# Gates of a hybrid decoder block computed by block products in a stage of their own, with three projections and the gated linear unit put in other places

## The chip, the cores and the metric

One core of a Trainium2 chip runs the whole program in a single launch. The metric is the device time of one execution in microseconds (us). The engines are named as the profile names them: PE (matrix multiply, with PEld for its weight loads), DVE (vector), ACT (scalar), POOL (GpSimd) and SP, which issues most of the transfers. Each engine works through its own queue in order.

## The reference, cut to what matters

One decoder block of width 1024 over 1024 tokens, in float32. After an RMS norm `u`, one projection gives the state space input, q, k, v, forget logits and two sets of gate logits:

```python
proj = u @ w_in[l]
u_ssm, q, k, v, f_logit, gate_logits = jnp.split(proj, [...], axis=-1)
y_ssm = jax.nn.gelu(s5_ssm(u_ssm, ...))                  # diagonal state space, 32 groups
glu_a, glu_b = jnp.split(y_ssm @ w_glu[l], 2, axis=-1)
out_a = glu_a * jax.nn.sigmoid(glu_b)
att = forgetting_attention(q, k, v, f_logit + b_forget)  # 8 heads of 64, causal
gate_a, gate_b = jnp.split(jax.nn.sigmoid(gate_logits), 2, axis=-1)
h = h + (gate_a * out_a + gate_b * (att @ w_fox_o)) @ w_mix_out
```

Then come a cross attention into 256 memory tokens, a gated feed-forward layer and a last norm, which the change leaves as they are.

## The kernel before, in words

Every matrix is held as a rounded high part and a low part (`split`, L172: ACT writes the high part, DVE subtracts it from the source for the low part), and a product is three matmuls, high by high, high by low and low by high (`mm3`, L161). A block of weights is 128x1024: it is loaded into `raw` (2 buffers) and split into `whi` and `wlo` (4 buffers each). The order of instructions on each engine is worked out when the program is built, by a list scheduler with a cost model; the order in the code is the priority. So an instruction may run ahead of its place in the code when its inputs and its buffer are free, and each engine's queue is then fixed.

The stages around the change:

1. `stage_in` (L327) norms the input, turns it into `uT` (transposed, high and low, 16 tiles of 128x1024), and stores the state space input `u_d`.
2. `stage_ssm` (L441) works the state space off in four quarters. For a quarter `weights` (L1161, POOL and DVE) builds tables, `turn_weights` (L1221) and `states` (L1245) run small matmuls on PE, a chain of DVE operations with two scans, and `out` (L1288) the last matmuls, a GELU on ACT and a split on DVE; `store` (L1305) sends the result to `y_d` in 16 transfers. Beside it PE computes the gates: 32 halves (16 blocks of 128 gates, 2 halves of 512 tokens, L447), each of 24 matmuls of 128x512, a sigmoid on ACT (L453) and a store to `gate_d` from ACT's queue (L454). `todo` (L460) says before which half each step of the state space stands.
3. `values_of_v` (L1328) projects v, 16 times 24 matmuls of 256 or 264 columns.
4. `run` (L1569): q and k of a head come from one weight block (`project`, L1425, 48 matmuls a head), those of heads 0 and 1 ahead of the loop, those of heads 2 to 7 between the 12 units (128 keys by up to 512 queries) of earlier heads. A unit does scores (L1508, L1509), the causal mask on DVE, the exponential on ACT (L1515), the split of the result (L1517 to L1521), and the products with v. `row_max` (L1466) finds the maxima of the next head on DVE. Beside head 7 run the first halves of the gated linear unit (`Glu.values`, L1004) for 4 of its 8 blocks.
5. `stage_tail` (L471) begins with the rest of the gated linear unit (`Glu.rest`, L1007: a product, a sigmoid on ACT, a product of both on DVE, L995, and one with the gate on POOL, L1002) and with `fox_part` (L493), the output projection of the attention, its gate and the sum. Then come mixing, cross attention and feed-forward.

The feed-forward layer already multiplies by seven block products (L719 to L804): two neighbouring 128-wide column blocks and two halves of the tokens make a 2x2 block product of which seven products of 12 matmuls each are taken in place of eight, with sums of weight blocks (`w_sums`, L740, on DVE) and of input blocks (`norm_blocks`, L686).

Memory is given out in pools that open and close like brackets. A pool that opens later lies where closed ones lay, and its tile waits for the last use of the tiles that lay there.

## Time and profile before

| | us |
|---|---|
| median of 3 runs (1609.87 to 1611.17) | 1610.64 |
| the profiled execution's own time | 1611.79 |
| its span in the profile | 1610.1 |
| busy: PE, DVE, ACT, POOL | 1543.0, 1019.0, 647.7, 254.6 |
| mean granted clock of PE | 0.982 |

The profile is of one execution. A table by windows gives for each stretch of time how long each engine was busy, the clock that PE was granted and how busy the transfer engines were. A group of instructions has a line, an engine, an operation, tiles (written from read), a shape, a count, and then busy time and mean duration. Matmuls are pipelined: a row may say 0.39 us for one while the next starts 0.23 us later, so time on PE is counted from start to start.

### The profile page before, as it was taken

How to read it: one execution, taken by the hardware profiler on the slowest of the kernel's cores; microseconds unless marked ns; L12 is line 12 of the kernel's file. 1: busy time of each engine (PE TensorE's matmuls, PEld its weight loads, DVE VectorE, ACT ScalarE, POOL GpSimd, SP SyncE). 2: the span in 40 equal slices, each digit the busy share in tenths (PEclk: the TensorE clock that was granted, in tenths of full speed). 3: DMA queues.
4: the chain of work that ended last, by engine and by line, in shares of the span. 5: the costliest groups of instructions: out<-in, count | busy, mean ns of one | idle time of the engine just before them, and what ended most of it. 6: DMA issues, size and time to landing. Idle time of an engine off the chain costs nothing.

```text
span 1610.1 us, 20541 instructions
## 1 busy us (share of the span) xinstructions
PE 1543.0 (96%) x7313; PEld 1267.3 (79%) x7313; DVE 1019.0 (63%) x1850; ACT 647.7 (40%) x1169; POOL 254.6 (16%) x339
## 2 busy tenths in 40 slices
PE   7799799998999999999999989999999999999997
PEld 6588688898677668888888776888888888888886
DVE  6655665424778776764355697776777667565555
ACT  6322333323566653222235574333333333344342
POOL 2025545100111112310001200000010000000001
PEclk8899999999899999999999999999999999999999
DMA  7746656633322453544203155444455544896642
GB/s 262 125 77 120 92 118 104 152 69 42 41 54 61 120 156 89 168 131 144 92 3 103 57 193 181 159 151 152 156 161 165 167 155 141 274 392 228 194 157 105
DMA packets 226102, 221.77 MB, mean 138 GB/s; under 512 B 50872, under 2 KB 159512, under 8 KB 226000
## 3 DMA queue, kind: packets, MB, share of 16 engines
q1 hardware_dynamic: 221392, 212.08, 47.1%
q10 hardware_dynamic: 4608, 8.39, 1.4%
q8 instruction: 57, 0.93, 0.2%
q14 instruction: 45, 0.37, 0.1%
HBM read 154.06 MB, written 64.32 MB: 136 GB/s over the span
## 4 chain that ended last, share of the span: by engine, by line
PE 79%; DVE 8%; DMA 6%; ACT 3%; POOL 2%; issue 2%; SPq 0%; DVEq 0%; POOLq 0%; ACTq 0%
PE mm L768 14%; PE pv L768 7%; PE mm L163 7%; PE mm L164 7%; PE mm L165 7%; PE mm L907 5%; PE sc L907 4%; PE sc L768 3%; DMA raw<-in_w_in_dram 3%; PE sc L163 3%; PE sc L165 3%; PE sc L164 3%; PE pv L907 3%; PE misc L907 2%; DVE wlo L174 1%
## 5 line engine op out<-in xcount | busy, mean ns | idle before, releaser
L174 DVE TENSOR_TENSOR wlo<-raw,whi 128x1024 fp32r<-128x1024 f32 (+2 forms) x126 | 133.2, 1059 | 179.6 <-ACT whi L173 166.9
L173 ACT CAST whi<-raw 128x1024 fp32r<-128x1024 f32 (+2 forms) x129 | 116.1, 903 | 303.5 <-DMA raw<-in_w_in_dram 67.9
L163 PE MATMUL mm<-uh,whi 128*128 128x512 f32 x344 | 139.9, 407 | 0.3 <-DVE mc L1486 0.3
L164 PE MATMUL mm<-ul,whi 128*128 128x512 f32 x344 | 137.9, 401 | 0.0
L165 PE MATMUL mm<-uh,wlo 128*128 128x512 f32 x344 | 137.6, 400 | 0.0
L174 DVE TENSOR_TENSOR ol<-or,oh 128x1024 fp32r<-128x1024 f32 x73 | 89.3, 1223 | 70.2 <-ACT oh L173 69.1
L173 ACT CAST oh<-or 128x1024 fp32r<-128x1024 f32 x73 | 76.8, 1053 | 103.7 <-PE mm L907 33.3
L800 POOL TENSOR_TENSOR g<-a,c 128x512 f32<-128x512 f32 x22 | 35.3, 1606 | 391.7 <-ACT a L799 357.4
L165 PEld LDWEIGHTS mm<-uh,wlo 128*128 128x128 f32 x344 | 66.6, 194 | 14.0 <-DVE wlo L174 0.7
L163 PEld LDWEIGHTS mm<-uh,whi 128*128 128x128 f32 x344 | 66.4, 193 | 12.8 <-DVE mc L1486 0.6
L164 PEld LDWEIGHTS mm<-ul,whi 128*128 128x128 f32 x344 | 66.5, 193 | 11.7
L1518 POOL TENSOR_TENSOR pl<-pf,ph 128x512 fp32r<-128x512 f32 (+1 forms) x32 | 36.9, 1153 | 236.6 <-DVE ph L1517 222.6
L192 POOL TENSOR_TENSOR r<-ms,mhalf 128x1 f32<-128x1 f32 x26 | 17.5, 672 | 359.0 <-DVE ms L188 350.7
L1515 ACT ACTIVATE pf<-sc 128x512 f32<-128x512 f32 (+1 forms) x96 | 46.4, 490 | 50.2 <-DVE sc L1511 35.1
L768 PE MATMUL pv<-S3h,we 128*128 128x512 f32 x176 | 58.9, 394 | 2.7 <-ACT S3h L173 2.7
L907 PE MATMUL mm<-oh 128*128 128x512 f32 x106 | 41.2, 389 | 0.0
L907 PE MATMUL mm<-ol,oh 128*128 128x512 f32 x106 | 41.2, 389 | 0.0
L907 PE MATMUL mm<-oh,ol 128*128 128x512 f32 x106 | 41.2, 389 | 0.0
L1521 DVE TENSOR_TENSOR pl<-pf,ph 128x512 fp32r<-128x512 f32 (+2 forms) x64 | 36.4, 571 | 7.6 <-ACT ph L1520 6.8
L768 PEld LDWEIGHTS pv<-S3h,we 128*128 128x128 f32 x176 | 33.3, 189 | 10.0 <-ACT S3h L173 3.1
L163 PE MATMUL sc<-uh,whi 128*128 128x512 f32 x104 | 40.8, 393 | 0.0
L1002 POOL TENSOR_TENSOR sg<-sg,ga 128x512 f32<-128x512 f32 x16 | 29.2, 1847 | 72.9 <-DVE sg L995 72.5
(574 smaller groups left out, 4556.5 us busy)
## 6 DMA issues: line engine op xcount, KB each, us to landing
or<-c_d SPq DMA_DIRECT2D x77, 256.0 KB
raw<-in_w_ffn_in_dram SPq DMA_DIRECT2D x22, 512.0 KB
rawb<-in_w_ffn_in_dram SPq DMA_DIRECT2D x22, 512.0 KB
wo<-in_w_ffn_out_dram SPq DMA_DIRECT2D x22, 512.0 KB
c_d<-g SPq DMA_DIRECT2D x44, 256.0 KB
t_d<-wo SPq DMA_DIRECT2D x44, 256.0 KB
or<-t_d SPq DMA_DIRECT2D x44, 256.0 KB
raw<-in_w_in_dram SPq DMA_DIRECT2D x20, 512.0 KB
```

Of the source, the lines that this page charges most:

```text
L163: T.matmul(ps, lh, rh, start=first, stop=False)
L164: T.matmul(ps, lh, rl, start=False, stop=False)
L165: T.matmul(ps, ll, rh, start=False, stop=last)
L173: self.A.copy(hi, src)
L174: (self.G if pool_lo else self.V).tensor_sub(lo, src, f32(hi))
L768: T.matmul(ps, l_[:, k, :], r_, start=first and k == 0 and i == 0, stop=k == 3 and i == 2, skip_group_check=True)
L800: G.tensor_mul(g[:, 512:], a1, c1)
L907: T.matmul(ps, l_[:, gi], r_[:, 512:], start=n < 3 and p == 0 and k == 0 or n == 7 and p == 0 and k == 0, stop=p == NP - 1 and k == 2, ski ...
L1002: self.B.G.tensor_mul(self.out[j][:, cs], self.out[j][:, cs], ga)
L1515: A.activation(pf[:, off:], ps[:, off:], AF.Exp)
L1518: G.tensor_sub(pl[:, off:], pf[:, off:], f32(ph[:, off:]))
L1521: V.tensor_sub(pl[:, off:], pf[:, off:], f32(ph[:, off:]))
```

## The change

The change does four things.

- **Beside the state space** run v (8 units of two token tiles) and then q and k (8 blocks by 2 halves of tokens). Their high and low parts go to memory (`vh_d`, `vl_d`, `q_d`, `k_d`) from SP's queue, and the attention loads them from there, per head and in two halves. The forget logits are summed at the end of this stage.
- **Gates** come after the state space in `stage_gates`, by seven block products per pair of blocks. The class `Seven` holds the weight side, taken over from the feed-forward layer, which now uses it too. `combine` makes the sums of the input blocks from `uT` in two parts.
- **The gated linear unit** of blocks 0 to 6 is cut into 112 steps of three matmuls: 16 ahead of the attention's loop and one in each of its 96 units. Block 7 comes after the attention. The results go to memory (`sg_d`) and are loaded in the tail.
- The loading of `y_d` moves into and behind the gates, and a few tiles share memory.

```diff
-    gates = [lambda j=j, h=h: gate(j, h) for j in range(16) for h in range(2)]
+    def value(b, t):
+        n = 264 if b else 256
+        ps = B.bank()
+        for k in range(8):
+            wh, wl = wv[b][k // 4]
+            B.mm3(ps[:, :n], *uT.tok(k, t), wh[:, k % 4, :], wl[:, k % 4, :], k == 0, k == 7)
+        hi, lo = parts()
...
+        A.copy(hv[:, :, 0:64], src)
+        V.tensor_sub(lo[:, :256].rearrange("p (h d) -> p h d", h=4), src, f32(hv[:, :, 0:64]))
+        S.dma_start(vh_d[t // 2, :, t % 2, 4 * b:4 * b + 4, :], f32(hv))
+        S.dma_start(vl_d[t // 2, :, t % 2, 256 * b:256 * b + 256], f32(lo[:, :256]))
+    def qk(i, hf):
+        ps = B.bank()
+        B.gemm_t(ps, *wq[i], uT, hf, 8)
+        hi, lo = parts()
...
+        for two in range(2):
+            d_ = (q_d, k_d)[i % 2][i // 2 * 2 + two]
+            h = slice(DH * two, DH * two + DH)
+            S.dma_start(d_[0:DH, cs], f32(first[h, :]))
+            S.dma_start(d_[DH:P, cs], f32(second[h, :]))
+    units = [lambda b=b, t=t: v_unit(b, t) for b in (1, 0) for t in range(0, NT, 2)]
+    units += [lambda i=i, hf=hf: qk_unit(i, hf) for i in range(8) for hf in range(2)]
     for q in range(4):
-        todo[4 + 7 * q] = [lambda q=q: s5.turn_weights(q)]
-        todo[5 + 7 * q] = [lambda q=q: s5.states(q, u_d)] + ([lambda q=q: s5.weights(q + 1)] if q < 3 else [])
-        todo[9 + 7 * q] = [lambda q=q: s5.out(q), lambda q=q: s5.store(q, y_d)]
+        t0 = (4, 10, 15, 21)[q]
+        todo.setdefault(t0, []).append(lambda q=q: s5.turn_weights(q))
+        todo.setdefault(t0 + 1, []).extend([lambda q=q: s5.states(q, u_d)] + ([lambda q=q: s5.weights(q + 1)] if q < 3 else []))
+        todo.setdefault(t0 + 5, []).extend([lambda q=q: s5.out(q), lambda q=q: s5.store(q, y_d)])
...
+    forget.log_forget()
+    forget.cumulate()
+def stage_gates(B, cp, gp, uT, w_in, gate_d, load_y):
+    def slot(dt=F32, name="w"):
+        return gp.tile([P, D], dt, tag="w", bufs=6, name=name)
...
+    def combine(k):
+        for n in ("A11", "A21", "A22"):
+            hi, lo = flat(n)
+            whole[n] = slot(name="f")
+            V.tensor_add(whole[n], f32(hi), f32(lo))
...
+        V.tensor_sub(s1, s1, s3)
+        V.tensor_sub(s3, t, s3)
+        V.tensor_add(t, t, s1)
+        put("S2", t, neg=True)
+        put("S3", s3)
+        put("S1", s1)
+        V.tensor_sub(s4, t, f32(hi))
+        V.tensor_sub(s4, s4, f32(lo))
+        put("S4", s4)
...
+    sv.fetch(0)
+    sv.first(0)
+    sv.fetch(1)
+    start(0)
+    combine(0)
+    sv.first(1)
+    start(1)
+    combine(1)
+    sv.sums(0)
+    sv.last(0)
+    middle(0)
+    end(0)
...
+    for j in range(2, 8):
+        start(j)
+        end(j - 1)
+        sv.last(j)
+        middle(j)
...
+    def steps(self, j, tile_, half):
+        def step(h, b, k):
...
+            B.mm3(ps, wh[:, 4 * b + k, :], wl[:, 4 * b + k, :], *self.yT.rhs(k, h), k == 0, k == 3)
+            if k < 3:
+                return
...
+            if b == 0:
+                B.V.tensor_copy(dst, pv)
+                return
+            sb = half("sb")
+            B.A.activation(sb, ps, AF.Sigmoid)
+            B.V.tensor_mul(dst, dst, sb.rearrange("p (t c) -> p t c", t=4))
...
+        steps = [f for j in range(7) for f in glu.steps(j, big, lambda name: big(name)[:, :512])]
+        weave(steps[:12], self.row_max(0))
+        self.max_row(0)
+        for f in steps[12:16]:
+            f()
+        steps = steps[16:]
...
             if h + 2 < NH:
-                n = 8 if h + 3 == NH else 16
-                for i, f in enumerate(pro[h + 2].parts[:n]):
-                    side[i if n == 8 else PSLOT[i]].append(f)
...
+                side[7].append(lambda: self.load(h + 2, (0,)))
+                side[11].append(lambda: self.load(h + 2, (1,)))
             for i, u in enumerate(units):
                 self.scores(h, *u)
                 for f in side[i]:
                     f()
+                steps.pop(0)()
```

In `put` each sum is split as everywhere, ACT the high part and DVE the low part. `start(j)` runs products 1 and 2 of a pair (inputs A11 and A12, which are `uT` itself), `middle(j)` products 6, 7 and 5 (inputs S2, S3, S1), `end(j)` products 3 and 4 (S4, A22).

499 lines of the change are left out of this document (268 added, 231 removed).

## The prediction

> **What bounds the kernel now.** First the page's engine table:
>
> ```profile
> span 1610.1 us, 20541 instructions
> ...
> PE 1543.0 (96%) x7313; PEld 1267.3 (79%) x7313; DVE 1019.0 (63%) x1850; ACT 647.7 (40%) x1169; POOL 254.6 (16%) x339
> ```
>
> PE is busy for 96% of the span, so a change pays by taking matmuls away or by closing PE's 67 us of idle time. The table by windows shows where these lie in the part that is changed. Its columns are window, length, busy time and count of PE, PEld, DVE, ACT and POOL, granted clock, share of the transfer engines, GB/s.
>
> ```profile
> 113.40:336.50 223.10, 213.96 (x1079) 182.57 (x1078) 112.22 (x150) 75.98 (x120) 100.53 (x201) 0.98 0.64 118
> 336.50:382.00 45.50, 45.09 (x374) 44.52 (x373) 18.27 (x61) 8.73 (x19) 1.64 (x5) 1.00 0.11 20
> 382.00:423.00 41.00, 35.28 (x136) 27.22 (x135) 20.92 (x46) 15.04 (x22) 0.00 (x0) 0.88 0.49 66
> 423.00:474.00 51.00, 49.73 (x245) 37.50 (x244) 38.26 (x98) 34.02 (x67) 9.19 (x8) 1.00 0.25 47
> 474.00:524.00 50.00, 49.45 (x240) 37.08 (x238) 39.76 (x102) 32.18 (x63) 9.24 (x8) 1.00 0.21 55
> 524.00:574.00 50.00, 46.19 (x225) 34.14 (x224) 38.86 (x101) 29.92 (x59) 9.23 (x8) 1.00 0.52 138
> 574.00:624.00 50.00, 47.74 (x228) 35.92 (x228) 36.55 (x71) 24.77 (x51) 9.24 (x8) 1.00 0.36 96
> 624.00:733.00 109.00, 109.00 (x483) 90.23 (x482) 79.18 (x83) 32.51 (x46) 29.20 (x16) 1.00 0.49 152
> ```
>
> These are gates beside the state space, v, the start of attention, its loop (four windows), and the tail to the end of the attention's output projection: 619.6 us. All else stays. The loss in each is idle time plus what the clock took: 9.1 + 0.02 x 214 = 13.4 us in the first, 5.7 + 0.12 x 35 = 9.9 in the third, 7.9 in the loop, nothing in the tail.
>
> The price of a matmul is the step from one start to the next, read from the chain that ended last:
>
> ```profile
> 1019.25 5.44 PE mm L768 x24
> ```
>
> Twenty-four matmuls of 512 columns take 5.44 us, 0.2267 us each. Matmuls of v, with half the columns, take 45.5 / 374 = 0.122 us.
>
> **The change part by part.**
>
> *Matmuls.* The gates fall from 16 x 2 x 24 = 768 matmuls to 8 x 7 x 12 = 672: 96 x 0.2267 = 21.8 us less on PE. v (384), q and k (384) and the gated linear unit (384) keep their counts and only move.
>
> *Beside the state space.* The first window holds 1079 matmuls: 768 for gates (174.1 us), 288 of the state space and 23 early ones of v (2.8 us); with 4.3 us for the clock, the state space takes 213.96 - 174.1 - 2.8 - 4.3 = 32.8 us of PE. After the change PE has, until the last quarter's `states` matmuls end, v (384 x 0.122 = 46.8), 14 of 16 halves of q and k (76.2) and the state space without its last `out` (29.3): 152.3 us. The stalls now:
>
> ```profile
> PE pv L1299 <- DVE St L1285: 5.5, 2, 5.3
> ...
> PE pv L1256 <- ACT F L1229: 3.6, 1, 3.6
> ```
>
> The first is the first quarter's DVE chain: the same number of units stands ahead of its `out`, a little longer ones, so it shrinks. The second comes with a crowded transfer queue:
>
> ```profile
> q10 hardware_dynamic: 4533, 8.27, 9.8%
> ```
> ```profile
> L1309 SPq DMA_DIRECT2D y_d<-yh x32: 302/432/4677, 190.7 to 330.2; - x32
> ```
>
> Queue q10 carried the gates' 32 stores from ACT. In their place SP gets 32 stores of v and 64 of q and k, 12.6 MB, at about 0.43 us an issue 41 us of its time, in a shorter stage. They stand in SP's queue among weight loads, the state space's transfers and `y_d`; a late one holds a `ph` or `pl` buffer (2 each), then ACT, then a PSUM bank. I take 10 us of stalls, between 3 (the first chain alone) and 25. Sum 162.3 us, against 223.1 with all the gates.
>
> *The start of the gates* is where the change pays. The last quarter of the state space, PE first, then DVE:
>
> ```profile
> 295.69 1.95 PE L1256 MATMUL pv<-xg,F 128*128 128x128 f32 x16
> ...
> 322.61 0.39 PE L1299 MATMUL pv<-St,Gm 128*128 128x128 f32 x2
> ```
> ```profile
> 311.09 0.68 DVE L1285 TENSOR_TENSOR St<-m,m 64x508 f32<-64x508 f32 x1
> ...
> 324.23 1.29 DVE L174 TENSOR_TENSOR yl<-m,yh 128x512 fp32r<-128x512 f32 x2 [2.67 <-ACT yh L173]
> ```
>
> From the end of `states` on PE (297.4) DVE needs 14.4 us to 311.8, `out` 3.5 us on PE (16 pairs at 0.22), its evacuation 2.8 us (322.7 to 325.5): 20.7 us. Today gates cover it. After the change only two halves of q and k (10.9 us) are left, and then DVE has to make the input sums before product 6 of any pair can run. Can it do so earlier? The pools `comb` and `gw` lie where those of the state space lay, about as large, and today's attention pool shows what that means:
>
> ```profile
> POOL vhi L1337 <- PE pv L1299: 15.1, 1, 15.1
> ```
>
> POOL had a tile of the next stage ready to write and waited 15.1 us for the last `out`. `combine` needs four of `gw`'s six large slots, so I let it start when the evacuation is done. Durations of what it runs (shape, count, busy, mean ns):
>
> ```profile
> L174 DVE TENSOR_TENSOR ol<-or,oh 128x1024 fp32r<-128x1024 f32 x73 | 89.3, 1223 | 70.2 <-ACT oh L173 69.1
> L174 DVE TENSOR_TENSOR wlo<-raw,whi 128x512 fp32r<-128x512 f32 x44 | 30.2, 685 | 5.1 <-ACT whi L173 4.4
> L777 DVE TENSOR_TENSOR a<-a,sc 128x512 f32<-128x512 f32 x22 | 14.9, 679 | 1.4 <-PE sc L768 1.1 <-issue 0.3
> ```
>
> Two calls of `combine` are 24 operations of 128x1024 at 1.2 us, 28.8; one split of pair 1, 1.2; seven operations of 128x512 in `sums` until product 6 has its weights, 4.8; two evacuations, 1.4: 36.2 us. From `states` to product 6 it is 20.7 + 36.2 = 57 us, and PE has 10.9 + 3.5 + 4 x 2.72 = 25.3 us of work for it: 32 us idle. Behind `combine` on DVE wait the sums of both weight pairs, and for these ACT's splits and PE. Bounds: 8 us idle, if slots come free so early that most of `combine` falls into DVE's gaps; 41, if the forget logits' 9 us of small operations stand ahead of it. I take 32: the row above decides. After such a gap PE is slow:
>
> ```profile
> 402.75 0.30 PE L1481 MATMUL mm<-hb 68*128 68x128 f32 x1 [3.90 <-issue]
> ...
> 406.17 0.63 PE L164 MATMUL mm<-ul,whi 128*128 128x512 f32 x1
> 406.60 0.63 PE L165 MATMUL mm<-uh,wlo 128*128 128x512 f32 x1
> ...
> 409.87 0.40 PE L1481 MATMUL mm<-hb 68*128 68x512 f32 x1
> ```
>
> After 3.9 us of idleness matmuls start 0.43 us apart instead of 0.23 for 7 us: about 3 us lost. The Trainium skill, "TensorE: Matmul & The Clock Gate", Part 1 (the HAM clock gate), says that a gap is followed by half the clock for about 3.4 us of work; by that the loss would be an estimated 1.7 us and the sum 1.3 lower.
>
> The other 52 products take 52 x 2.72 = 141.4 us; per pair DVE has some 10 us beside 19, and the feed-forward layer ran so without loss.
>
> *Start and loop of attention.* The windows from 382 to 624 are 242 us with 480 of the moved matmuls (q, k and a quarter of the gated unit); after the change 112 x 3 = 336. PE busy 228.4, less 4.2 for the clock, less 144 x 0.2267 = 32.6, is 191.6. The waits were 17.8 us. What the engines beside PE gain and lose:
>
> ```profile
> L989 DVE COPY sg<-mm 128x512 f32<-128x512 f32 x16 | 17.9, 1151 | 5.2 <-PE mm L165 4.8
> L995 DVE TENSOR_TENSOR sg<-sg,sb 128x512 f32<-128x512 f32 x16 | 21.0, 1325 | 8.7 <-ACT sb L994 8.6
> L1457 DVE SCALAR_TENSOR_TENSOR hb<-mm,hb 64x512 fp32r<-64x512 f32 x16 | 10.9, 684 | 6.8 <-ACT hb L1456 6.3
> L1455 ACT ACTIVATE hb<-mm 64x512 fp32r<-64x512 f32 x16 | 9.4, 590 | 5.4 <-PE mm L165 5.1
> L994 ACT ACTIVATE sb<-mm 128x512 f32<-128x512 f32 x10 | 5.9, 594 | 10.6 <-PE mm L165 7.6 <-POOL sg L1002 3.1
> L994 ACT ACT_TABLE_LOAD x1 | 1.3, 1283 | 0.0
> ```
>
> DVE loses 32 evacuations like L1457 (22 us), 12 splits (15) and 8 copies (9), and gains for seven blocks two copies, two products and a split each (43 us): 174 us before, 172 after, in a shorter time, so its share goes from 72% to 82%. ACT loses 64 evacuations and 12 splits (50 us) and gains 14 sigmoids, splits and, since each of the 12 sigmoids in the loop stands among exponentials, up to 24 table loads of 1.28 us (31): 136 before, 133 after. The scores run two units ahead, which covers one burst of two loads. The start no longer waits for a late weight block, but for 1.5 MB of q and k of head 0, 4.2 MB of v and the maxima of head 0 on DVE, with 10.9 us of steps to cover them. I leave the waits at 17.8, between 8 (the loop without its start) and 36 (double): 209.4 us.
>
> *Tail.* Block 7 (48 matmuls, 10.9 us) and the output projection (192, 43.5) replace 109 us. The last head's result lands late:
>
> ```profile
> L1567 SPq DMA_DIRECT2D atl<-alo x4: 462/528/598, 610.7 to 637.5; - x4
> ```
>
> The last store of it is issued 13.5 us after the loop and takes some 2 us to land; block 7 and the products that do not need it cover about 13.5: 2 us, plus 2 for the reloaded results. Bounds 0 and 10: 58.4 us.
>
> *The sum:* 162.3 + 57 + 3 + 141.4 + 209.4 + 58.4 = 631.5 us in place of 619.6: 12 us more. On the profiled execution's own time, 1611.79, that is 1623.7; it lies 1.15 above the median of the runs, so on that scale 1622.6, and I forecast 1623.
>
> **Rivals.**
>
> 1. *The input sums are hidden.* If the scheduler finds slots free early, `combine` runs in DVE's gaps (DVE is busy for half of the first window) and 24 of the 32 us and the slow clock go: 1623 - 24 - 1 = 1598. For it: part of the pool is free well ahead; POOL wrote other tiles of the attention before its wait. Against it: the waiting row, and four slots are needed at once. This is the case in which the kernel gets faster; it decides from 20 us hidden on.
> 2. *Attention becomes bound by ACT and DVE.* If bursts of two table loads and a sigmoid are not covered, waits double: 1623 + 18 = 1641. What speaks against it is that DVE and ACT stay under 85%. The trace shows the load right behind the copy ahead of it:
>
> ```profile
> 623.82 0.58 ACT L1542 COPY num<-pv 65x512 f32<-65x512 f32 x1 [2.95 <-PE pv L1540]
> 624.42 1.28 ACT L994 ACT_TABLE_LOAD   x1
> ```
>
> The copy ends at 624.40 and the load starts at 624.42, so 1.28 us is all that is seen. The Trainium skill, "ScalarE: Activation LUTs", section "What ACT_TABLE_LOAD costs", adds about 1.38 us for draining to each load. By that rule the 24 loads would cost ACT an estimated 33 us more, and with half of it uncovered the time would be 1639.
>
> 3. *Transfers choke the first stage*: 96 more issues on SP and some 80% use of the transfer engines raise its stalls to 25 us: 1638.
> 4. *It balances*: the first stage runs with 3 us of stalls and the attention with 13 of waits: 1623 - 7 - 5 = 1611.
>
> That seven products do not take the place of eight would need 96 matmuls more in the count; the code leaves no room for it.
>
> **How the numbers follow.** Forecast 0.50, hidden sums 0.15, attention 0.15, transfers 0.10, balance 0.10. A measurement of this kernel tells about 0.2%, 3.2 us, from no change. Faster: the first rival and a little of the fourth, 0.16; within 0.2%: most of the fourth, 0.09; slower: 0.75. The forecast's own range is 1614 to 1634. The range given, 1600 to 1640, leaves out the lower half of the first rival and the upper half of the second, some 0.16.
>
> **What would show it.** Right: PE idle for 25 to 40 us in one stretch between `out` of the last quarter and product 6 of pair 0, with DVE busy throughout; the rest of the gates at 2.72 us a product; fewer than 7313 - 90 matmuls. Wrong: that stretch under 15 us, `combine` running before the last `out`; a loop of attention over 205 us; PE waiting for weights or banks beside the state space.

## The result and the profile after

The changed kernel takes 1727.51 us (median of 4 runs, 1726.36 to 1731.75) against 1610.26 for the kernel before on the same chip: a ratio of 1.0734, interval 1.0713 to 1.0756. It is slower, as forecast, but by 117 us and not by 12, and lies far above the range of 1600 to 1640. The profiled execution took 1728.65 us. Its engine table:

```profile
span 1726.9 us, 20850 instructions
...
PE 1559.3 (90%) x7217; PEld 1268.6 (73%) x7217; DVE 1087.0 (63%) x1954; ACT 674.9 (39%) x1199; POOL 251.8 (15%) x351
```

7313 - 7217 = 96 matmuls are gone, exactly those of the forecast, and yet PE is busy for longer and idle for 168 us instead of 67. The table by windows of the changed kernel, cut at the ends of the forecast's terms (the last row is all that the change leaves alone; columns as in the prediction):

```profile
111.30:321.60 210.30, 177.48 (x1049) 159.07 (x1047) 104.31 (x167) 50.03 (x96) 93.53 (x207) 0.90 0.66 121
321.60:380.10 58.50, 14.74 (x65) 11.54 (x65) 49.13 (x78) 15.42 (x24) 3.85 (x3) 0.62 0.49 92
380.10:549.80 169.70, 150.01 (x600) 119.66 (x601) 78.54 (x111) 62.94 (x99) 0.95 (x1) 0.91 0.53 110
549.80:593.50 43.70, 38.14 (x136) 27.71 (x136) 24.37 (x57) 11.60 (x16) 6.46 (x9) 0.84 0.75 236
593.50:780.10 186.60, 171.30 (x813) 123.68 (x812) 148.49 (x341) 120.83 (x211) 53.60 (x42) 0.99 0.49 144
780.10:849.70 69.60, 58.85 (x239) 46.43 (x239) 46.00 (x60) 19.47 (x29) 6.77 (x4) 0.90 0.62 192
849.70:1726.90 877.20, 856.63 (x3876) 704.98 (x3875) 562.04 (x899) 348.73 (x643) 68.09 (x62) 0.99 0.49 160
```

The last row took 877.1 us before. So the whole loss is in the six rows above it:

| term of the forecast | forecast | measured | off by |
|---|---|---|---|
| beside the state space | 162.3 | 210.3 | +48.0 |
| start of the gates, up to product 6 (57 + 3) | 60.0 | 58.5 | -1.5 |
| the other 52 products | 141.4 | 169.7 | +28.3 |
| start and loop of attention | 209.4 | 43.7 + 186.6 = 230.3 | +20.9 |
| tail | 58.4 | 69.6 | +11.2 |
| sum | 631.5 | 738.4 | +106.9 |

The only term near its size is the one on which the forecast dwelt. The rows are cut in time, and some work lies in another row than the forecast put it. The first row holds 1049 matmuls where the forecast had 976: the last two halves of q and k and 24 matmuls of the gates, 16.3 us at 0.2267, run ahead of the last `states` and are missing in the second row. The third row holds 600 of its 624 matmuls. The attention's two rows have 25 matmuls of the gates and 3 of block 7 besides, 6.3 us.

In these rows PE is not busy for 738.4 - 610.5 = 127.9 us, against 619.6 - 596.4 = 23.2 before. The waits of PE in the changed kernel (line that waits, what ended the wait; total, times, longest) say where the long ones are:

```profile
PE mm L605 <- ACT whi L172: 37.7, 2, 30.6
PE mm L605 <- ACT c L683: 13.9, 3, 7.8
PE pv L1469 <- DMA xg<-u_d: 10.6, 2, 8.4
PE mm L162 <- ACT whi L172: 9.6, 1, 9.6
PE pv L162 <- DMA ath<-ahi: 6.9, 1, 6.9
```

Of the first, 30.6 us are the idle stretch that was forecast. In the second the gates wait for ACT's copy out of the PSUM bank to which the next product adds. The third is the state space waiting for its own input, the fourth a weight block of q or k, the fifth the last head's result. The five make up 79 of the 128 us. The rest are shorter waits, and PE's clock is lower among them (0.90, 0.91 and 0.90 in the long rows of the stage, the gates and the tail).

### The profile page after: what moved, and what is told of

It is laid out like the page before. It is cut to its first block, busy times and chain, and to the rows that moved or that the text cites. A ratio compares the mean times of both kernels' runs of the same rounds, so it can differ in the third digit from the quotient of the medians.

```text
span 1726.9 us, 20850 instructions
## 1 busy us (share of the span) xinstructions
PE 1559.3 (90%) x7217; PEld 1268.6 (73%) x7217; DVE 1087.0 (63%) x1954; ACT 674.9 (39%) x1199; POOL 251.8 (15%) x351
## 4 chain that ended last, share of the span: by engine, by line
PE 59%; DVE 14%; DMA 11%; issue 5%; POOL 4%; ACT 3%; SPq 3%; DVEq 0%; POOLq 0%; ACTq 0%
PE mm L605 16%; PE pv L605 8%; DMA raw<-in_w_in_dram 5%; PE mm L1111 4%; PE sc L605 3%; PE mm L162 3%; PE sc L1111 3%; PE mm L164 3%; PE mm L163 3%; PE pv L1111 3%; PE misc L1111 2%; DMA xt<-in_x_dram 2%; PE sc L162 1%; PE sc L164 1%; PE sc L163 1%
## 5 line engine op out<-in xcount | busy, mean ns | idle before, releaser
L172 ACT CAST whi<-raw 128x512 fp32r<-128x512 f32 (+2 forms) x137 | 117.7, 861 | 323.0 <-DMA raw<-in_w_in_dram 90.5
L173 DVE TENSOR_TENSOR wlo<-raw,whi 128x512 fp32r<-128x512 f32 (+2 forms) x134 | 132.7, 992 | 175.6 <-ACT whi L172 174.4
L605 PE MATMUL mm<-S,whi 128*128 128x512 f32 x128 | 42.9, 417 | 36.2 <-ACT whi L172 30.6
L162 PE MATMUL mm<-uh,whi 128*128 128x512 f32 x144 | 59.7, 415 | 9.6 <-ACT whi L172 9.6
L162 PE MATMUL mm<-yh,whi 128*128 128x512 f32 x128 | 54.0, 422 | 5.2 <-DVE sg L1203 2.5
L163 PE MATMUL mm<-ul,whi 128*128 128x512 f32 x144 | 58.5, 407 | 0.0
L164 PE MATMUL mm<-uh,wlo 128*128 128x512 f32 x144 | 58.5, 406 | 0.0
L605 PEld LDWEIGHTS mm<-S,whi 128*128 128x128 f32 x128 | 25.3, 200 | 43.5 <-ACT whi L172 31.0
L163 PE MATMUL mm<-yl,whi 128*128 128x512 f32 x128 | 52.0, 406 | 0.0
L164 PE MATMUL mm<-yh,wlo 128*128 128x512 f32 x128 | 51.5, 403 | 0.0
L162 PEld LDWEIGHTS mm<-uh,whi 128*128 128x128 f32 x144 | 28.8, 200 | 15.6 <-ACT whi L172 9.8
```

What stands on the lines that cost most here:

```text
L162: T.matmul(ps, lh, rh, start=first, stop=False)
L163: T.matmul(ps, lh, rl, start=False, stop=False)
L164: T.matmul(ps, ll, rh, start=False, stop=last)
L172: self.A.copy(hi, src)
L173: (self.G if pool_lo else self.V).tensor_sub(lo, src, f32(hi))
L605: self.B.T.matmul(ps, l_[:, k, :], r_, start=first and k == 0 and i == 0, stop=k == 3 and i == 2, skip_group_check=True)
```

## The experiments

The times below are medians with the ratio to the kernel before on the same chip. Stretches are those of the table, each from one profiled execution: "stage" is 111.3 to 321.6, "start" the next row, and so on. Builds with an untouched loop gave loops of 185.7 to 191.1 us, so a difference of under 5 us there says little.

### Beside the state space

**Is it PE's work or the chain of the state space?** `e14_thin_projections`:

```diff
-        for k in range(8):
-            wh, wl = wv[b][k // 4]
-            B.mm3(ps[:, :n], *uT.tok(k, t), wh[:, k % 4, :], wl[:, k % 4, :], k == 0, k == 7)
+        wh, wl = wv[b][1]
+        B.mm3(ps[:, :n], *uT.tok(7, t), wh[:, 3, :], wl[:, 3, :], True, True)
...
-        B.gemm_t(ps, *wq[i], uT, hf, 8)
+        B.mm3(ps, wq[i][0][:, 7, :], wq[i][1][:, 7, :], *uT.rhs(7, hf), True, True)
```

> v, q and k are computed from one eighth of the input: 672 of their 768 matmuls are left out, some 107 of 123 us of PE in the first stage; splits, weight loads, stores and the state space stay. Theory A (the first stage is as long as the chain of the state space and the stores, 40 to 50 us a quarter, and PE's work only lies beside it): from its start to the end of the last `states` it takes 165 us or more, against 210. Theory B (PE's work and its stalls add up, as the forecast did it): it falls to 110 to 130 us. The whole follows: above 1680, or 1627 to 1650.

Measured: 1727.2 us (1.0718, 1.07 to 1.0736). 672 matmuls (336 of v at 0.122 us and 336 of q and k at 0.2267, 117 us of PE) are gone and the time is the same: the stage takes 208.5 us in place of 210.3. Its windows, cut at the ends of the quarters' `states` matmuls:

```profile
111.30:141.20 29.90, 11.44 (x65) 10.30 (x63) 10.11 (x17) 7.10 (x15) 17.90 (x48) 0.62 0.70 142
141.20:185.70 44.50, 23.73 (x106) 20.30 (x105) 37.90 (x55) 14.97 (x29) 32.87 (x66) 0.64 0.43 99
185.70:266.30 80.60, 27.23 (x109) 22.14 (x109) 40.47 (x59) 13.69 (x25) 31.30 (x57) 0.59 0.63 125
266.30:319.80 53.50, 25.83 (x99) 19.90 (x99) 25.19 (x38) 15.44 (x29) 13.99 (x38) 0.69 0.72 130
```

PE is busy for 88 us of 208.5. Only DVE in the second quarter (37.9 of 44.5) comes near to full, so what sets the stage is mostly a chain of waits. The granted clock is lower here (0.59 to 0.69), so part of the chain can be slower matmuls. By these clocks they are some 32 of the 88 us, an estimate; were all of that in the chain, 176 us would be left. How the chain was hidden is in the kernel before, second to fourth quarter:

```profile
145.20:205.30 60.10, 50.96 (x242) 43.42 (x241) 40.98 (x53) 18.10 (x30) 37.21 (x63) 0.91 0.63 95
205.30:251.50 46.20, 46.20 (x241) 39.52 (x241) 25.52 (x36) 15.72 (x26) 23.81 (x49) 1.00 0.58 122
251.50:297.60 46.10, 46.10 (x241) 39.45 (x240) 23.12 (x37) 16.98 (x27) 18.69 (x42) 1.00 0.72 121
```

and in the third and fourth quarter of the changed kernel:

```profile
202.80:271.90 69.10, 60.67 (x305) 51.82 (x304) 31.74 (x47) 12.69 (x26) 28.45 (x53) 0.92 0.55 104
271.90:321.60 49.70, 36.76 (x177) 30.66 (x176) 24.04 (x37) 12.26 (x23) 12.54 (x38) 0.84 0.79 130
```

Before, PE was busy without a gap in the last two quarters and gave each 46 us, whatever the chain needed. Only the second, 60.1 us with 9.1 idle, let something of it show. The forecast's 162.3 us allows 40.6 a quarter on average. The third quarter now takes 69.1, and SP's queue in the changed kernel shows it (start, us on the queue, line):

```profile
213.65 0.60 SPq L508 DMA_DIRECT2D k_d<-ph  x1
235.93 0.45 SPq L507 DMA_DIRECT2D k_d<-pl  x1
...
255.95 4.75 SPq L1456 DMA_DIRECT2D Tt<-W  x7
...
263.31 0.59 SPq L1462 DMA_DIRECT2D xg<-u_d  x1
```

together with DVE's:

```profile
222.38 1.22 DVE L173 TENSOR_TENSOR wlo<-raw,whi 128x1024 fp32r<-128x1024 f32 x1
230.15 0.29 DVE L1424 TENSOR_TENSOR d<-EC,trg_cs 128x128 f32<-128x128 f32 x1 [6.55 <-POOL ES L1426]
...
235.21 0.68 DVE L173 TENSOR_TENSOR pl<-mm,ph 128x512 fp32r<-128x512 f32 x1
```

DVE first has the state space's own operations (209.1 to 222.3), then waits 6.55 us for POOL, which begins the next quarter's tables, works on them until 235.2, and only then makes the low part `pl` of a half of q or k. SP stands from 214.3 to 235.9 at the store of that `pl`, with everything behind it: further stores, `y_d`, the transfers of `Tt` (a table of weights), and last `xg`, the input of the next `states`, which leaves 27 us after the queue moves again. So three things are in the chain: tables, `pl`, and the order of SP's queue. The following runs take them apart.

**Another queue for the stores.** `e1_act_stores`:

```diff
-            S.dma_start(d_[0:DH, cs], f32(first[h, :]))
-            S.dma_start(d_[DH:P, cs], f32(second[h, :]))
+            A.dma_start(d_[0:DH, cs], f32(first[h, :]))
+            A.dma_start(d_[DH:P, cs], f32(second[h, :]))
```

(and the two stores of v in the same way).

> The 96 stores of v, q and k are issued from ACT instead of SP; nothing else changes. Theory A (SP's queue, which works in order, is what stretches the first stage: a store that waits for its split holds up the state space's loads and the weight loads behind it): the first stage, from 111.3 us to the end of the last `states` matmuls, falls from 210 us to 165 to 180, and the whole to 1683 to 1698. Theory B (the state space's own chain with single buffers for Tt, xg and F, or the two buffers of ph and pl, sets the pace whichever queue issues): the first stage stays at 200 us or more and the whole above 1717.

Measured: 1737.4 us (1.0781, 1.0765 to 1.0797), 10 us slower than the changed kernel; the stage takes 209.8 us. The wait has only moved: ACT now has the stores in its own queue, and PE waits for ACT's other work, which is not among the long waits of the changed kernel:

```profile
PE pv L1441 <- ACT m L1515: 14.5, 2, 11.5
```

On SP or on ACT, the stores cost the stage the same; a third queue was not tried. The 10 us lie behind the stage: the start of the gates takes 65.8 us in place of 58.5, the loop 191.0 in place of 186.6.

**Fewer, larger stores.** `e6_two_stores`:

```diff
-        for two in range(2):
-            d_ = (q_d, k_d)[i % 2][i // 2 * 2 + two]
-            h = slice(DH * two, DH * two + DH)
-            S.dma_start(d_[0:DH, cs], f32(first[h, :]))
-            S.dma_start(d_[DH:P, cs], f32(second[h, :]))
+        d_ = (q_d, k_d)[i % 2][i // 2 * 2:i // 2 * 2 + 2]
+        for r, t_ in enumerate((first, second)):
+            S.dma_start(d_[:, DH * r:DH * r + DH, cs], f32(t_))
```

> Each half of q or k is stored by two transfers of 128 rows instead of four of 64 rows: 32 issues on SP fewer, the same bytes and the same waits. Theory A (SP issues back to back at about 0.6 us from 236 to 270 us and again before 320 us, so its rate is the limit there): 19 us of issue time go, the last `states` ends 8 to 19 us earlier and the whole is 1708 to 1720. Theory B (the wait of the first store for its split is what costs, not the issues): less than 5 us, the whole above 1722.

Measured: 1811.06 us (1.1237, 1.1219 to 1.1254), the worst of all; the stage takes 276.8 us. The same bytes in half as many stores hold SP's queue for 78.8 us in place of 41.3, half of them for 2.4 us or more (first row below: some of this run's, minimum/median/maximum in ns; second row: the changed kernel's):

```profile
L506 SPq DMA_DIRECT2D q_d<-pl x8: 485/2104/8242, 188.0 to 368.1; - x8
```
```profile
L507 SPq DMA_DIRECT2D q_d<-ph x16: 451/587/1221, 189.3 to 313.2; - x16
```

From 236 to 262 us the transfer engines are busy for 47% and move 64 GB/s where the changed kernel has 73% and 131. The Trainium skill, "DMA: Bandwidth & Descriptors", section "Why a DMA increments its semaphore by 16 and not by 1", says that a transfer is spread over the largest number of engines up to 16 that divides the slowest dimension above size 1 of both its sides. Here that dimension became 2 in memory. The slow stores agree with that, but no run varied the dimension alone. As a test of the number of issues this run failed; it shows that what a slow store holds up, the stage pays for.

**No stores.** `e5_no_stores` drops the lines with `S.dma_start` of `value` and `qk`, and lets the attention read bytes of `y_d`:

```diff
-        S.dma_start(vh_d[t // 2, :, t % 2, 4 * b:4 * b + 4, :], f32(hv))
-        S.dma_start(vl_d[t // 2, :, t % 2, 256 * b:256 * b + 256], f32(lo[:, :256]))
...
-            S.dma_start(d_[0:DH, cs], f32(first[h, :]))
-            S.dma_start(d_[DH:P, cs], f32(second[h, :]))
```

> The stores of v, q and k are left out, with their splits kept; the attention reads as many bytes of y in their place, so its result means nothing. Moving the stores to ACT left the first stage at 210 us, but it put ACT's queue behind the same splits, so it did not tell whether the stores matter. Theory A (stores that wait in an order, on whichever queue, and hold the state space's transfers and weight loads up are what stretches the stage): the end of the last `states` matmuls falls from 321.6 us to 275 to 288 and the whole to 1682 to 1695. Theory B (the state space's own chain, with POOL's tables built in place and single buffers, sets the pace without them): it stays above 305 us, the whole above 1711.

Measured: 1717.61 us (1.0655, 1.0635 to 1.0675). The stage takes 189.7 us, 20.6 less: neither nothing nor all. (The start of the gates gives back 7.5 of it.) The bytes go with the issues, so the run does not tell waiting in the queue from traffic. In the changed kernel's third quarter the transfer engines are busy for 55%, which speaks for the queue but does not show it.

**No tables.** `e9_tables_kept` uses the first quarter's tables in all four:

```diff
+        if q:
+            return
         EC, ES = [t2(n).rearrange("p (j c) -> p j c", j=4) for n in ("EC", "ES")]
```

> The state space's rotation tables (EC, ES and r8) are built for the first quarter alone and kept for the other three, which leaves their own tables out; all stores stay. Theory A (the tables have one buffer, so each quarter POOL builds them for 10 us after the states' scan, DVE then doubles them for 6 us, ACT waits 12 us with the copy of r8, and the splits and stores of q and k stand behind all that): the last `states` ends at 280 to 300 us instead of 321.6, the whole 1690 to 1708. Theory B (SP's queue alone delays the states): above 312 us, the whole above 1717.

Measured: 1722.47 us (1.0692, 1.0676 to 1.0708), stage 204.4 us, 5.9 less. So the tables alone are not it either.

**Neither.** `e10_no_stores_tables` has the edits of the last two.

> Both left out: the stores of v, q and k, and the tables of quarters 2 to 4. Theory A (these two make up the whole excess of the first stage over the forecast): the last `states` ends at 272 to 282 us, where the forecast had 275.7, the whole 1670 to 1685. Theory B (what is left of the quarter's chain, with Tt, xg and F in one buffer and a weight block fetched one ahead, sets the pace by itself): above 290 us, the whole above 1695.

Measured: 1700.18 us (1.0552, 1.0534 to 1.0569). The stage takes 174.8 us, 35.5 less, more than the two alone (26.5); the whole is 27.3 us shorter. Third and fourth quarter:

```profile
205.90:246.10 40.20, 36.99 (x194) 31.95 (x193) 25.59 (x32) 12.91 (x24) 18.39 (x19) 0.96 0.69 73
246.10:287.00 40.90, 40.90 (x217) 35.10 (x217) 20.68 (x28) 11.15 (x21) 5.37 (x5) 1.00 0.41 68
```

With both gone PE is full or nearly so again in these two, at the 40.6 us that the forecast allowed. Not all of the 35.5 us is gained: the stage holds 982 matmuls in place of 1049, the others stand behind `states` again, and the start of the gates takes 64.4 us. The two rows together are 222.3 us in the forecast, 268.8 in the changed kernel and 239.2 here, so tables and stores make up 29.6 of the 46.5 us. What is left of the stage lies in the second quarter (146.6 to 205.9, 59.3 us, about as long as before the change). There PE waits 10.6 and 2.6 us for DVE's `pl`, and DVE has, beside the state space, some 13 us of the forget logits, which this build's order puts into that quarter. That these are the cause was not tested.

### The start of the gates

**Is it the input sums?** `e4_no_input_sums` leaves `combine` out:

```diff
     start(0)
-    combine(0)
     sv.first(1)
     start(1)
-    combine(1)
+    for n in ("S1", "S2", "S3", "S4"):
+        sv.comb[n] = sv.comb["A11"]
```

> The input sums of the gates are left out: the products that want them read A11 instead, so 24 operations of 128x1024 on DVE and 8 splits on ACT are gone. Theory A (PE's gap of 30.6 us before product 6 is the input sums on DVE, as the prediction's third step has it): the gap falls to 3 to 8 us, the whole to 1700 to 1706. Theory B (the forget logits' chain on DVE and the late second weight block of pair 0 hold product 6 up as well, one behind the other): the gap stays above 12 us and the whole above 1709.

Measured: 1713.88 us (1.0634, 1.0616 to 1.0651). The start takes 43.5 us in place of 58.5, and the idle stretch 15.7 in place of 30.6: half of it goes. What is left is a transfer, the row of DVE's first weight sum in this run:

```profile
363.64 0.69 DVE L581 TENSOR_TENSOR raw<-raw,rawb 128x512 f32<-128x512 f32 x1 [7.29 <-DMA rawb<-in_w_in_dram]
```

The changed kernel has the same wait, covered by `combine`. Its DVE, and its SP queue:

```profile
353.28 3.48 DVE L633 TENSOR_TENSOR f<-uh,ul 128x1024 f32<-128x1024 f32 x3
360.94 0.69 DVE L581 TENSOR_TENSOR raw<-raw,rawb 128x512 f32<-128x512 f32 x1 [4.18 <-DMA rawb<-in_w_in_dram]
```
```profile
344.88 3.72 SPq L1522 DMA_DIRECT2D y_d<-yl  x8
...
352.67 1.02 SPq L564 DMA_DIRECT2D rawb<-in_w_in_dram  x2
```

`combine` begins at 353.28, 31.7 us after `states`, and not after 20.7. Ahead of it DVE has the forget logits (335.3 to 352.1, with the last splits of `yl` between).

**Is it the forget logits?** `e8_forget_early` moves them forward:

```diff
+    todo[21] += [forget.log_forget, forget.cumulate]
...
-    forget.log_forget()
-    forget.cumulate()
```

> The forget logits and their running sum are placed behind the last quarter's `turn_weights` instead of behind the whole first stage, so that DVE, POOL and PE do them before the last quarter's states and not between its `out` and the input sums. Theory A (they hold the input sums up, as the trace has them, one behind the other from 335 to 352 us): product 6 of pair 0 starts 9 to 13 us earlier after the last `states`, 46 to 50 us instead of 58.5, the whole 1714 to 1719. Theory B (the input sums wait for the slots of the last quarter's tiles or for the late second weight block anyway): less than 4 us, the whole above 1723.

Measured: 1730.69 us (1.0735, 1.0706 to 1.0764), start 58.1 us: no gain, and `combine` begins 32.3 us after `states`. With DVE free, it waits for the last stores of the state space:

```profile
351.61 0.69 DVE L670 TENSOR_TENSOR a<-a,sc 128x512 f32<-128x512 f32 x1 [5.56 <-DMA y_d<-yl]
```

So two things hold the start of `combine` at about the same time, the logits on DVE and memory that `y_d`'s stores still read. The forecast let it begin with the evacuation; the stores follow that.

### The other products of the gates

In the changed kernel the second block of a pair's weights, `rawb`, is fetched into one of the six `w` slots of `gw`, and `raw` stands behind it in SP's queue. That queue, ACT, which splits the block, and the longest of SP's waits from 380 to 550 us:

```profile
426.57 0.37 SPq L564 DMA_DIRECT2D raw<-in_w_in_dram  x1
451.31 0.37 SPq L564 DMA_DIRECT2D rawb<-in_w_in_dram  x1
452.51 0.37 SPq L564 DMA_DIRECT2D raw<-in_w_in_dram  x1
```
```profile
439.54 1.04 ACT L172 CAST whi<-raw 128x1024 fp32r<-128x1024 f32 x1 [11.40 <-DMA raw<-in_w_in_dram]
461.55 1.05 ACT L172 CAST whi<-raw 128x1024 fp32r<-128x1024 f32 x1 [7.47 <-DMA raw<-in_w_in_dram]
```
```profile
SPq L564 <- DVE wdl L173: 106.0, 10, 24.2
```

ACT stands idle for `raw`, 11.4 and 7.5 us, and SP stands 106 of 170 us at these fetches until DVE has made `wdl`, a low part, of an earlier pair, which frees the slot. The fetch is not ahead of the work; it follows the slot that the work frees.

**Other memory for it.** `e2_rawb_big` puts `rawb` of pairs 2 to 7 into tiles of `big` that are free until the attention, and loads `y_d` after the last fetch:

```diff
-               lambda: slot(name="rawb"), slot)
+               lambda: big.tile([P, D], F32, tag="big", name="rawb") if late else slot(name="rawb"), slot)
...
     sv.last(1)
+    late.append(1)
     sv.fetch(2)
...
-    load_y(0)
     for j in range(2, 8):
...
+    load_y(0)
     end(7)
```

> In the gates the second raw weight block of pairs 2 to 7 lies in the four tiles of the normed input that the input sums have used up, not among the six large slots of the gates' own pool; the first half of y is loaded after the last weight block instead. Theory A (the weight block of the next pair is fetched late because it waits for a slot, and the fetch behind it on SP waits with it): the rest of the gates, from product 6 of pair 0 to the first product of the gated linear unit, falls from 170 us to 145 to 152, and the whole to 1702 to 1712, less a few us if the gated linear unit then waits for y. Theory B (the load itself or the splits on ACT and DVE are too slow for 19 us a pair): it stays above 165 us, the whole above 1722.

Measured: 1710.36 us (1.062, 1.0599 to 1.0642). The stretch falls from 169.7 to 150.3 us, and no other of the six rows moves by more than 1.3:

```profile
378.70:529.00 150.30, 143.02 (x601) 115.38 (x602) 78.66 (x111) 62.42 (x100) 0.96 (x2) 0.95 0.57 130
```

So 19.4 us were slots. The row holds 601 matmuls, 136.2 us at 0.2267: of the 14.1 us left, 7.3 are idle time and 6.8 slower matmuls.

### The loop of the attention

**Table loads.** `e3_exp_for_sigmoid` takes an exponential in place of the sigmoid of the gated unit, so that ACT keeps its table:

```diff
-            B.A.activation(sb, ps, AF.Sigmoid)
+            B.A.activation(sb, ps, AF.Exp)
```

> The gated linear unit applies an exponential where the sigmoid stood, so that ACT keeps one table in the attention's loop: the sigmoid is left out, everything else stays. Theory A (the 22 table loads of 1.28 us, 28 us of ACT, are what doubles PE's waits in the loop): the loop from 590 to 780 us gets 13 to 18 us shorter, the whole 1709 to 1715. Theory B (DVE, busy for 83% of the loop, sets the pace, and ACT's loads are covered): less than 5 us, the whole above 1722.

Measured: 1725.62 us (1.0704, 1.0679 to 1.0728). The loads of the changed kernel in the whole attention were

```profile
L1660 ACT ACT_TABLE_LOAD x11 | 14.1, 1283 | 0.2
L1206 ACT ACT_TABLE_LOAD x11 | 14.1, 1283 | 0.2
```

and of these 22 only one is left. The loop takes 187.0 us in place of 186.6, the total 1.9 us less, and the intervals overlap. 27 us less on ACT are worth next to nothing here. The Trainium skill, "ScalarE: Activation LUTs", section "What ACT_TABLE_LOAD costs", adds about 1.38 us of draining to each load; if it is there, it is covered too.

**DVE's part.** `e7_dve_relief` moves 28 copies and products of the gated unit off DVE, all but the splits:

```diff
-                B.V.tensor_copy(dst, pv)
+                B.A.copy(dst, pv)
...
-            B.V.tensor_mul(dst, dst, sb.rearrange("p (t c) -> p t c", t=4))
+            B.G.tensor_mul(dst, dst, sb.rearrange("p (t c) -> p t c", t=4))
```

> In the gated linear unit the copy of the first half from PSUM goes from DVE to ACT and the product with the sigmoid from DVE to POOL: some 25 us of DVE's 155 in the attention's loop go, ACT gains some 9. Theory A (DVE, busy for 83%, paces the loop): the loop of 187 us gets 8 to 16 us shorter, the whole 1711 to 1720. Theory B (PE's short waits come from the interleaving of three-matmul steps with scores and products on few PSUM banks, whoever empties them): less than 4 us, the whole above 1723.

Measured: 1722.1 us (1.0686, 1.0664 to 1.0708), loop 181.9 us, start 40.6. A few us at most. **Both** are in `e11_relief_exp`:

> The gated linear unit with its copy on ACT, its product on POOL (25 us less on DVE, which by itself gave 4.7 us of the loop) and an exponential for the sigmoid (no table loads; by itself 0 us): the sigmoid is left out. Theory A (ACT and DVE form one chain, so that either alone gives little and both together most): the loop of 186.6 us falls to 165 to 175, the whole to 1706 to 1716. Theory B (neither paces the loop; PE waits on the order of short steps among few banks): the loop stays at 179 us or more, the whole above 1718.

Measured: 1727.05 us (1.0719, 1.0702 to 1.0737), loop 191.3 us. The loop is no shorter with ACT and DVE relieved together, so the gain of `e7_dve_relief` is not secure either.

**PE's part.** `e13_thin_steps` issues only every fourth step's matmuls of blocks 0 to 6 of the gated unit:

```diff
-            B.mm3(ps, wh[:, 4 * b + k, :], wl[:, 4 * b + k, :], *self.yT.rhs(k, h), k == 0, k == 3)
+            if k < 3 and j < 7:
+                return
+            B.mm3(ps, wh[:, 4 * b + k, :], wl[:, 4 * b + k, :], *self.yT.rhs(k, h), k == 0 or j < 7, k == 3)
```

> Of the gated linear unit's blocks 0 to 6, which run beside the attention, only every fourth step issues its three matmuls; copies, sigmoids, products, loads and stores stay. So 252 matmuls, 57 us of PE at 0.2267, are left out, about 49 of them in the loop. Theory A (the loop's pace is no longer set by PE: the attention's own round trips over DVE, ACT and two PSUM banks make it some 180 us, whatever PE has besides): the loop of 186.6 us stays above 172 us, the whole above 1705. Theory B (PE's work and scattered waits add up): the loop falls to 137 to 150 us, the whole to 1665 to 1685.

Measured: 1726.95 us (1.0718, 1.0701 to 1.0734). The loop takes 183.7 us:

```profile
597.90:781.60 183.70, 153.72 (x633) 104.80 (x632) 151.69 (x341) 120.95 (x212) 54.18 (x42) 0.85 0.51 149
```

180 fewer records of matmuls in the loop, 41 us at 0.2267, make it 3 us shorter. But the granted clock falls from 0.99 to 0.85, so slower matmuls eat some 0.15 x 153.7 = 23 us of it, and this does not show that PE's work is free. The rest turns into idle time, 30.0 us in place of 15.3: something beside PE holds the loop up too.

**The mask.** In the loop ACT's longest wait is that of the exponential for the causal mask, which DVE adds. The changed kernel, and the kernel before:

```profile
ACT pf L1660 <- DVE sc L1656: 30.0, 30, 3.7
```
```profile
ACT pf L1515 <- DVE sc L1511: 31.5, 25, 2.9
```

`e17_mask_after` adds it by a matmul of 128 columns (`self.ones` holds the identity and the mask), and `e18_mask_before` does the same to the kernel before:

```diff
-        T.matmul(ps[:, off:], K2[:, k], Q2[:, q], start=False, stop=True)
         if kt * P >= 512 * qc:
-            V.tensor_add(ps[:, off:off + P], ps[:, off:off + P], self.trk)
+            T.matmul(ps[:, off:off + P], *self.ones, start=False, stop=False, skip_group_check=True)
+        T.matmul(ps[:, off:], K2[:, k], Q2[:, q], start=False, stop=True)
```

> The kernel after, with the causal mask of the diagonal blocks added by a matmul of 128 columns into the scores' bank instead of by DVE: 64 additions (18 us) go from DVE, 64 short matmuls (about 0.1 us each) come to PE. ACT's largest wait in the loop was for this addition (30 of 187 us), and it stands between each score and its exponential. Theory A (the loop's pace is the round trip score, addition, exponential over two PSUM banks): the loop of 186.6 us falls to 168 to 178, the whole to 1709 to 1719. Theory B (the round trip over the products' splits or the row maxima, or PE itself, paces it): 182 us or more, the whole above 1722.

> The same edit in the kernel before, whose loop of 197 us is 96% busy on PE and lost some 8 us to waits, 4.7 of them for exponentials. If that wait goes through the addition, 3 to 6 us of the loop go, less some 5 us of added matmuls on a PE that is nearly always busy: 1607 to 1613, hardly to be told from 1610. Theory A would allow a gain of up to 3 us, theory B a loss of up to 5.

Measured: 1728.98 us (1.0731, 1.0708 to 1.0753) and 1615.13 (1.0022, 1.0012 to 1.0033). The loop goes to 191.2 us in the one, at the edge of the scatter named above, and from 197.2 to 202.7 in the other. The wait is still there under another name; in the changed kernel with the mask on PE:

```profile
ACT pf L1663 <- PE sc L1659: 37.0, 32, 3.6
...
DVE pl L1669 <- ACT ph L1668: 21.3, 21, 2.9
```

What paces the loop stays open after these six runs.

### The tail

Of the last head, the changed kernel stores the sums (`rc`), then their reciprocals (`rd_d`), loads these spread out (`rb`), and stores the result (`ath`, `atl`), all on SP:

```profile
783.04 0.52 SPq L1696 DMA_DIRECT2D rc<-num  x1
...
792.82 0.32 SPq L1213 DMA_DIRECT2D sg_d<-sg  x1
793.24 0.47 SPq L1700 DMA_DIRECT2D rb<-rd_d  x1
...
802.29 1.10 SPq L1712 DMA_DIRECT2D atl<-alo  x2
```

These last stores leave 22.2 us after the loop (780.1), some 13 us before the change. PE waits from 795.3, 6.9 us, for `ath`. Each step is later than in the kernel before: `rc` leaves 2.9 us after the loop (0.6 before), `rd_d` 4.2 after `rc` (2.2 before), `rb` 6.0 after `rd_d` (1.5 before), and from `rb` to `ath` it is 6.8 as before. In the queue stand `sg_d`'s store ahead of `rb` and reloads of `sg` between.

**Order of the queue.** `e15_late_results` issues the reloads of blocks 2 to 6 after the last store, and `rb` comes ahead of `sg_d`:

```diff
+        glu.after = fox.last_store.ins
...
-    for j in range(2, 7):
-        fox_get(j)
+    with B.tc.issue_after(glu.after):
+        for j in range(2, 7):
+            fox_get(j)
```

> The reload of the gated linear unit's results 2 to 6 from memory is issued behind the last store of the last head instead of ahead of it on SP; in the same order the broadcast of the last head's reciprocals comes ahead of the store of block 6. Theory A (in the tail the last head's three round trips over memory wait behind 512 KB loads and a store that waits for POOL): from the loop's end to the last product of the output projection 62 to 65 us instead of 69.6, the whole 1720 to 1724. Theory B (the round trips take their 20 us for another reason): 68 us or more, the whole above 1725.

Measured: 1729.24 us (1.0734, 1.0706 to 1.0761), tail 66.7 us, 2.9 less, but the whole is no shorter than the changed kernel. `rb` now leaves 3.3 us after `rd_d`; the steps ahead of it are as late as they were, and what holds them was not tested.

### Together

`e12_four` has `e2_rawb_big` and `e7_dve_relief`, the store of `sg_d` on POOL's queue, and one copy of the tables on DVE:

```diff
-        A.copy(r8v, self.r8[:, j4].unsqueeze(2).to_broadcast([P, 4, P]))
+        V.tensor_copy(r8v, self.r8[:, j4].unsqueeze(2).to_broadcast([P, 4, P]))
...
-                    B.S.dma_start(self.sg_d[j * P:(j + 1) * P, :], cur["out"])
+                    B.G.dma_start(self.sg_d[j * P:(j + 1) * P, :], cur["out"])
```

> Four edits that lie in four stages, read by stage: r8 copied by DVE instead of ACT (first stage), the weight blocks of the gates in free tiles of the input (gates), copy on ACT and product on POOL in the gated linear unit (loop), and its results stored from POOL's queue instead of SP's (tail, where the last head's broadcast stood 5 us behind such a store on SP). By theory: `states` 4 to 10 us earlier, since ACT's wait of 12 us a quarter goes; the rest of the gates 17 us shorter; the loop 5 us shorter; from the loop's end to the last product of the output projection 64 to 66 us instead of 69.6; together 1690 to 1702. If ACT's wait is not on the path, the first edit gives nothing: 1698 to 1704. If POOL's own queue delays the store or the loads behind, the tail stays at 69 us or more.

Measured: 1707.93 us (1.0602, 1.0576 to 1.0627). Only the gates' edit pays (151.4 us); the stage (212.4), the loop (185.5) and the tail (69.1) do not move.

`e16_gates_and_tail` has the edits of `e2_rawb_big` and `e15_late_results`.

> The two edits that keep the result and that each theory of its stage supports, together: the weight blocks of the gates in free tiles of the input, and the late reload of results in the tail. They lie in different stages, so they should add: 17 us and 4 to 7, the whole 1702 to 1708; if the tail's edit gives nothing, 1709 to 1712. Neither is enough to come near the kernel before.

Measured: 1705.51 us (1.0585, 1.0567 to 1.0603): gates 150.3, tail 66.1. This is the fastest version of the change that keeps all its work, 22 us better than the change and 94 us behind the kernel before. Nothing here points to a version that beats that one.

## Why the prediction was right or wrong

**Matmuls: right.** 96 are gone, and the rest of the kernel is unmoved.

**Beside the state space: wrong, by 48 us, and it is the step of 152.3 us of matmuls plus 10 of stalls that failed.** It took PE's work as the length of the stage and added waits. But beside a chain, the length is the longer of the two, and the profile before hardly showed the chain's: PE was full at 46 us in the last two quarters, and only in the second, 60.1 us with 9.1 idle, did it come to light. The forecast read these as 5.5 us that shrink and 3.6 that come from the transfer queue. `e14_thin_projections` shows that even with an eighth of the projections' work the stage stays at 208.5. By PE, the 48 us are 16.3 of work that the forecast had behind `states`, 22.8 more idle (32.8 for 10), and 8.9 of slower matmuls. The 96 stores were counted as 41 us of SP's time, and that was near enough: those of v take 0.37 us and those of q and k 0.59 in the median, 32 x 0.37 + 64 x 0.59 = 50. But their stalls were bounded at 25 us with all else; what they cost the stage is 20.6 alone and more with the tables. In the third quarter the trace shows how: a store waits for its `pl` and holds the next quarter's `xg` behind it. Rival 3 named the right place and was short of it: 15 us over the forecast in place of 48. The mark set for this, PE waiting beside the state space, was met.

**Start of the gates: right in size, 58.5 for 60, idle 30.6 for 32 in one stretch, and partly by luck, as errors cancel.** `combine` began 11 us late, held by the forget logits (the upper bound that I had set aside) and by the stores of `y_d` (not thought of). In exchange the sums of pair 0's weights went ahead of most of the second `combine`, so that product 6 came 26.8 us after its start and not 36.2. DVE was not busy throughout, it also waited 4.2 us for `rawb`. And PE is in all idle for 43.8 us of this row, since 16.3 us of the work meant to fill it had been done. Input sums are worth 15 us by `e4_no_input_sums`. Rival 1, that they are hidden, is out.

**The other products: wrong, by 28.3 us.** The step that failed is "the feed-forward layer ran so without loss". I carried over DVE's load and not the slots. The row holds 600 matmuls, 136.0 us at 0.2267, so it loses 33.7 us: 19.7 idle and 14.0 of slower matmuls. `e2_rawb_big` shows 19.4 us of this to be slots; the rest was not taken apart.

**Attention: wrong, by 20.9 us, with the waits at the forecast's place.** The term "I leave the waits at 17.8" is the one that was too small. 191.6 us of work leave 38.7 us. Of these, 6.3 are matmuls of the gates and of block 7 that lie in this row, so the waits are 32.4, inside the bound of 36. By the two windows, as the forecast reckoned them, idle time and clock are 5.6 + 0.16 x 38 + 15.3 + 0.01 x 171 = 28.7; the other 3.7 are counted as busy and not explained. The size is near that of rival 2 (waits doubled, 18 us more), but its mechanism fell: the loads of tables cost nothing, and neither ACT and DVE relieved nor the mask moved to PE shortens the loop. How much of the loop PE's own work sets stays unknown, because the clock fell with the work. The cause is open.

**Tail: wrong, by 11.2 us.** Beside 54.4 us of work it took 4 us of waits, at most 10; waits and slower matmuls took 15.2. The last store was taken as 13.5 us after the loop, as before; it came after 22.2. `e15_late_results` brings 2.9 back.

Direction and the one mechanism on which the forecast was built held; it found a tenth of the loss, 12 of 117 us. The range was narrow because each bound was drawn from waits seen before, in a kernel whose PE covered everything behind it.

## What to carry to other kernels

When work moves to stand beside a chain of small steps, compare it with the chain's own length in each period and take the longer, and do not read that length from a profile in which the engine beside it is full. For every transfer that is added, ask what stands behind it on its in-order queue while it waits for its data, and for every fetch, which slot it needs and when that slot comes free: these are distances and not shares of time. A wait that has many causes does not go when one goes; take two away together before you call a suspect cleared.

## What the runs showed of the hardware

- 117 us of matmuls can leave a kernel without any change in time (1727.51 to 1727.2), and the granted clock falls with them (mean 0.945 to 0.915; in the loop with fewer steps 0.99 to 0.85).
- Half as many stores of twice the size made the stage 66.5 us longer; they held the queue for 78.8 us in place of 41.3, the longest for 8.2 in place of 2.3.
- Of 22 loads of ACT's tables, 28.2 us of its time, 21 could go without an effect that these runs can tell.
